# A two-layer decoder trunk: a second buffer for gathered token rows, the returned rows joined earlier, a fixed GpSimd order, and no filler matmuls

## The chip, the cores and the metric

The kernel runs on one core of a Trainium2 chip. Its time is the device time of one execution in microseconds (us). The engines of the core are named as the profile names them: PE is TensorE (matmuls; PEld its weight loads), DVE is VectorE, ACT is ScalarE, POOL is GpSimd, SP is SyncE. Each engine works through its own list of instructions in order, and an instruction waits on semaphores that other engines or DMA transfers raise.

## What is computed

Two layers over 256 tokens of width 1024, all in float32. Each layer mixes tokens (layer 0: a gated linear recurrence and attention to a fixed memory; layer 1: stick-breaking attention and the same kind of memory attention), then applies a mixture of experts; after each half comes a residual and a LayerNorm:

```python
for layer in range(2):
    mixed = concatenate([seq_out, mem_out])                 # token mixing
    x = layer_norm(ALPHA * x + mixed @ w_o[layer])
    # experts: a group of 4 is chosen, then 2 experts of its 4
    h = silu(x @ w_gate) * (x @ w_up)                       # 16 experts, 1024 -> 256
    y = einsum('tef,efd->td', h * gates[:, :, None], w_down)
    x = layer_norm(ALPHA * x + y)
```

## The kernel before

All weights lie in one table of 1 MB chunks. SP issues one DMA per chunk in a fixed order into a ring of buffers; further buffers join the ring where other tiles die (`stream.open(names, end)`; "o1" is one of them). PE has nearly always something to multiply, so the other engines' work is placed beside it.

**Experts.** `Moe.run` goes through 16 experts in eight pairs, p = 0 to 7, with 64 slots for tokens per expert, so a pair fills 128 rows. For each pair: the rows of its tokens are there (pair 0: made by matmuls; pairs 1 to 7: fetched from a copy `zd` of the normalised tokens in DRAM by an indirect DMA on POOL, L633, into the single tile `zg`); PE turns them (L743, tile `xgp`); `gu` multiplies them by the gate and up weights (L762); ACT and DVE form `h` (L809, L811); PE turns `h` (L832, tile `ht`); `po` multiplies by the down weights (L846). The results of pairs 0 to 4 (p < AWAY) go to a DRAM table `hd` by an indirect DMA on POOL (L716, "send"), those of pairs 5 to 7 are kept in `hl` and put to their tokens by matmuls (L771, tile `y`). When pair 6 is at work, each token's rows are read back from `hd` (L711, "bring"): its first into `r`, its second into `second`, 128 tokens at a time; both tiles are set to zero before, and POOL adds them (L803). After pair 7 DVE joins `r` to the residual (L868), and the last norm begins with `y` added to it (L366).

**A branch.** Between `h` and `ht` of pair 7 stands a test whether an expert has more than 64 tokens (`beyond`, L456). The engines all pass through it; the code in it is not run with these inputs. After the test PE waits for DVE's count that stands behind DVE's last instruction ahead of the test, as the trace names it `DVEq L456`.

**Order.** Inside the stages DVE, PE and ACT follow the program's order. On POOL a scheduler places the instructions that are not pinned. Before the first partition broadcast (L353, of a norm's gain and bias to all partitions) and before the first arithmetic instruction after one, POOL's list holds an instruction "ISA" which the trace calls MODIFY_POOL_CONFIG.

**The ends of the token mixing.** `mixer_end` normalises the tokens, stores them to `zd` from ACT's DMA queue (both halves), and computes who goes where; then `idx`, and the first `fetch`. `keep_busy` puts matmuls of no use on PE: 18 at the start of the program, 2, 4 and 4 at the end of layer 1's mixing, 11 between the layers (`into_next`). In layer 0's mixing, DVE doubles a decay table level by level (`double`, L1120 to L1122) and splits weights (`ag`, L220), and PE makes scores of blocks of 128 (L1165).

Of the kernel before, what the change touches and what calls it, by code (L numbers as in the profile page):

```python
# [7 lines left out]
F32 = mybir.dt.float32  # L8
# [34 lines left out]
def trunk(ctx: ExitStack, tc: tile.TileContext, w_all, x_tok_d, cst_d, msk_d, rw_d, rb_d,  # L43
# [87 lines left out]
    def keep_busy(ps, n):  # L131

        for _ in range(n):
            tc.keep_in_program_order(nc.tensor.matmul(ps, onesb, onesb[:, None, :].to_broadcast([P, 4, P]), start=True,
                                                      stop=True, skip_group_check=True))

# [50 lines left out]
    class Parts:  # L187


        def __init__(self):  # L190
            self.use("wa", "wb", "wd")

# [24 lines left out]
        def lo(self, p, src, j, scale=None):  # L217
            s = slice(j * 512, (j + 1) * 512)
            if scale is None:
# [128 lines left out]
    def rows(which, name):  # L348
# [3 lines left out]
        for v in range(2):  # L352
            nc.gpsimd.partition_broadcast(gb[:, v], gb[0:1, v])  # L353
# [45 lines left out]
    def affine(dst, z, gb, norms=None):  # L399

        for t in range(NT):
# [105 lines left out]
    class Moe:  # L507
# [16 lines left out]

        def turn_in(self, s, t, hk):
# [90 lines left out]
        def indices(self):  # L616
# [10 lines left out]

            self.zg = self.work.tile([P, D], F32, tag="zg", name=f"zg{l}")
            nc.gpsimd.memset(self.zg, 0.0)
            self.fetch(1)  # L630

        def fetch(self, p):
            nc.gpsimd.indirect_dma_start(out=self.zg, out_offset=None, in_=self.zd,  # L633
# [76 lines left out]
        def bring(self, dst, i, t):  # L710
            nc.gpsimd.indirect_dma_start(out=dst, out_offset=None, in_=self.hd,  # L711
                                         in_offset=bass.IndirectOffsetOnAxis(ap=self.back[:, i, t:t + 1], axis=0),
                                         bounds_check=ROWS - 1, oob_is_err=False)

        def send(self, p, src):
            nc.gpsimd.indirect_dma_start(out=self.hd, out_offset=bass.IndirectOffsetOnAxis(ap=self.own[:, p:p + 1], axis=0),  # L716
                                         in_=src, in_offset=None, bounds_check=ROWS - 1, oob_is_err=False)
# [19 lines left out]
        def transpose_rows(self, p):  # L737
            l = self.l
            xg = self.work.tile([P, NK, P], F32, tag="xg", name=f"xg{l}", bufs=2)
            for hk in range(2):  # L740
                ps = bank(f"xgp{l}", tag="m", shape=(P, 4, P))
                for k in range(4):
                    pin(nc.tensor.transpose(ps[:, k], self.zg[:, (4 * hk + k) * P:(4 * hk + k + 1) * P], ident))  # L743
# [4 lines left out]
        def run(self, x1, xg):  # L748
# [25 lines left out]
            def rows_of_next(p):  # L774
                xgs[p] = self.transpose_rows(p)
                if p < 7:
                    self.fetch(p + 1)

            for p in range(8):
# [33 lines left out]
                if p == 0:  # L813
                    self.turn(1)
                    hr = keep.tile([P, 2, D], F32, tag="u", name=f"hr{l}")
# [9 lines left out]
                if p == 7:  # L825
                    beyond(pool, self.pool, l, base, x1, self.most, self.late, y)
# [40 lines left out]
            for t in range(NT):  # L867
                nc.vector.scalar_tensor_tensor(x1[:, t], x1[:, t], ALPHA, r[:, t], op0=ALU.mult, op1=ALU.add)  # L868
# [756 lines left out]
```

## Time and profile before

| | |
|---|---|
| median of 3 runs | 535.89 us (532.68 to 543.47) |
| the profiled execution | 537.7 us, its span 535.9 us |
| mean granted TensorE clock | 0.983 |
| PE busy | 500.2 us (93% of the span) |
| DVE, ACT, POOL busy | 288.5, 228.5, 82.5 us |
| DMA | 158.88 MB, 296 GB/s mean |

Since PE is busy for 93% of the span, the profile is read from PE's timeline: each row there begins with a start time, and a bracket at its end gives PE's idle time just before it and who ended that. From there one goes to the timeline of the engine that ended it.

### The profile page before, as it was taken

Reading aid. Unit: us, or ns where it says so; the run is one execution under the profiler, and the core shown is the slowest. Engines: PE = TensorE matmul, PEld = TensorE weight load, DVE = VectorE, ACT = ScalarE, POOL = GpSimd, SP = SyncE. Lnnn points to the kernel's source line nnn. Section 1 sums busy time; section 2 is a strip of 40 time slices with the busy share of each in tenths; the row PEclk is TensorE's granted clock in tenths of the full one; section 3 lists DMA queues with packets and bytes.
Section 4 is the critical chain, followed back from the end, with each engine's and each line's share of the span. In section 5 each row is a group of like instructions: output and inputs, shape, how many; then the busy total and the mean of one; then the engine's idle time right before and its main releaser. Section 6 shows DMA issues by size and latency. Waiting matters only on the chain. (4 is left out here: it accounts for less than half of the span.)

```text
span 535.9 us, 9133 instructions
## 1 busy us (share of the span) xinstructions
PE 500.2 (93%) x3549; PEld 325.8 (61%) x3549; DVE 288.5 (54%) x667; ACT 228.5 (43%) x469; POOL 82.5 (15%) x90
## 2 busy tenths in 40 slices
PE   8999998999999889998998999999999779999992
PEld 4998898787995323333435889877787223333431
DVE  3668886657668322222138698676438522222236
ACT  4855436665453222222217565667424222222312
POOL 1100000002211101115331400000021111213431
PEclk9999999999999799999899999999999999999997
DMA  7999733354789999999985854334789999999602
GB/s 274 402 420 423 292 128 126 144 215 179 294 330 396 422 406 419 419 390 404 402 335 206 285 226 158 111 125 161 309 322 368 406 391 398 419 412 420 243 3 78
DMA packets 28009, 158.88 MB, mean 296 GB/s; under 512 B 5347, under 2 KB 5731, under 8 KB 11060
## 3 DMA queue, kind: packets, MB, share of 16 engines
q1 hardware_dynamic: 20736, 140.76, 66.3%
q10 hardware_dynamic: 2616, 8.74, 4.4%
q0 software_dynamic: 4608, 8.73, 4.3%
q8 instruction: 30, 0.49, 0.4%
q14 instruction: 19, 0.16, 0.1%
HBM read 157.88 MB, written 13.63 MB: 320 GB/s over the span
## 5 line engine op out<-in xcount | busy, mean ns | idle before, releaser
L762 PE MATMUL gu<-w,xg 128*64 128x512 f32 x512 | 119.9, 604 | 0.1
L762 PEld LDWEIGHTS gu<-w,xg 128*64 128x64 f32 x512 | 33.4, 137 | 56.3 <-issue 51.0
L846 PE MATMUL po<-w,hT 128*64 128x512 f32 x256 | 60.2, 610 | 0.1
L591 DVE TENSOR_SCALAR xg<-xgp,lnT 128x128 f32<-128x128 f32 x64 | 25.3, 409 | 51.6 <-ACT xg L593 50.2
L593 ACT ACTIVATE xg<-xgp,lnT 128x128 f32<-128x128 f32 x64 | 27.4, 457 | 55.8 <-PE xgp L743 52.0
L846 PEld LDWEIGHTS po<-w,hT 128*64 128x64 f32 x256 | 17.9, 139 | 35.2 <-issue 28.7
L853 DVE COPY hr<-po 128x512 f32<-128x512 f32 x10 | 6.9, 690 | 43.1 <-PE po L846 43.0
L743 PEld LDWEIGHTS xgp<-cst,zg 128*128 128x128 f32 x112 | 13.3, 152 | 20.0 <-issue 13.3
L633 POOL DMA_INDIRECT zg<-zd,idx x14 | 14.9, 1061 | 60.0 <-PE xgp L743 23.9
L743 PE MATMUL xgp<-cst,zg 128*128 128x128 f32 x112 | 16.7, 297 | 6.9 <-DMA zg<-zd,idx 6.7
L1215 POOL TENSOR_TENSOR rms<-rms,neghalf 128x2 f32<-128x2 f32 x6 | 4.1, 697 | 113.0 <-DVE rms L1214 113.0
L809 ACT ACTIVATE h<-gu 128x256 f32<-128x256 f32 (+1 forms) x18 | 6.3, 359 | 34.5 <-PE gu L762 34.5
L811 DVE SCALAR_TENSOR_TENSOR h<-gu,gsl,h 128x256 f32<-128x256 f32 (+1 forms) x18 | 8.0, 453 | 22.6 <-ACT h L809 22.6
L833 ACT ACTIVATE hT<-ht 128x256 f32<-128x256 f32 (+1 forms) x18 | 6.5, 360 | 31.4 <-PE ht L832 31.3
L220 DVE TENSOR_TENSOR wo<-w,wo 128x512 fp32r<-128x512 f32 x20 | 13.6, 717 | 11.0 <-ACT wo L215 11.0
L353 POOL PARTITION_BROADCAST gbm<-gbm x4 | 5.0, 1307 | 93.9 <-DMA gbm<-in_ln_dram 86.4
L851 DVE TENSOR_TENSOR hl<-po,hl 128x512 fp32r<-128x512 f32 x12 | 8.2, 689 | 20.9 <-ACT hl L850 20.9
L716 POOL DMA_INDIRECT hd<-hr,own x10 | 10.5, 1052 | 52.8 <-DVE gsl L735 47.4
L855 ACT ACTIVATE hr<-po 128x512 f32<-128x512 f32 x10 | 6.0, 597 | 23.5 <-PE po L846 23.5
L850 ACT ACTIVATE hl<-po 128x512 fp32r<-128x512 f32 x12 | 7.1, 597 | 20.7 <-PE po L846 12.9
L215 ACT ACTIVATE wo<-w 128x512 fp32r<-128x512 f32 x20 | 11.6, 629 | 9.7 <-PE wo L439 8.8
L771 PE MATMUL y<-hl,PT 128*128 128x512 f32 x48 | 14.3, 419 | 1.4 <-DVE hl L851 1.4
(458 smaller groups left out, 1329.4 us busy)
## 6 DMA issues: line engine op xcount, KB each, us to landing
w<-in_w_all_dram SPq DMA_DIRECT2D x131, 1024.0 KB, 8.1
hd<-in_w_all_dram ACTq DMA_DIRECT2D x2, 2560.0 KB, 21.6
zd<-s ACTq DMA_DIRECT2D x4, 512.0 KB, 9.1
w<-in_w_all_dram SPq DMA_DIRECT2D x6, 256.0 KB, 5.8
x_tok<-in_x_tok_dram ACTq DMA_DIRECT2D x1, 1024.0 KB, 4.8
out_dram<-z SPq DMA_DIRECT2D x4, 256.0 KB, 2.0
w<-in_w_all_dram SPq DMA_DIRECT2D x1, 512.0 KB
cst<-in_cst_dram SPq DMA_DIRECT2D x1, 233.0 KB, 10.7
```

The costliest lines, as they stand in the source:

```text
L215: self.last_hi = nc.scalar.activation(p[:, 0, s], src[:, s], AF.Copy, scale=1.0 if scale is None else scale).ins
L220: nc.vector.tensor_sub(p[:, 1, s], src[:, s], p[:, 0, s])
L591: nc.vector.tensor_scalar(xg[:, kk], ps, g, b, op0=ALU.mult, op1=ALU.add)
L593: nc.scalar.activation(xg[:, kk], ps, AF.Identity, scale=g, bias=b)
L633: nc.gpsimd.indirect_dma_start(out=self.zg, out_offset=None, in_=self.zd, in_offset=bass.IndirectOffsetOnAxis(ap=self.idx[:, p:p + 1], axi ...
L716: nc.gpsimd.indirect_dma_start(out=self.hd, out_offset=bass.IndirectOffsetOnAxis(ap=self.own[:, p:p + 1], axis=0), in_=src, in_offset=None ...
L743: pin(nc.tensor.transpose(ps[:, k], self.zg[:, (4 * hk + k) * P:(4 * hk + k + 1) * P], ident))
L762: pin(nc.tensor.matmul(gus[p][c * 64:(c + 1) * 64], xgs[p][:, kk, c * CAP:(c + 1) * CAP], ws[p][2 * kh + c][0][:, k * 512:(k + 1) * 512], ...
L771: pin(nc.tensor.matmul(y[t][h], self.PT[p][:, t], hl[:, i, s], start=(p == AWAY and i == 0), stop=(p == 7 and i == 1)))
L811: nc.vector.scalar_tensor_tensor(h[:, c], gus[p][:, 256 + c.start:256 + c.stop], self.gsl[:, p:p + 1], h[:, c], op0=ALU.mult, op1=ALU.mult)
L846: pin(nc.tensor.matmul(po[c * 64:(c + 1) * 64], hT[:, f, c * 64:(c + 1) * 64], ws[p][4 + c][0][:, f * D + hf * 512:f * D + hf * 512 + 512] ...
L851: nc.vector.tensor_sub(hl[:, 1, s], po, hl[:, 0, s])
```

## The change

- `zg` becomes two tiles of rows, made as soon as the tokens are stored. `fetch(1)` and `fetch(2)` are issued together, and `fetch(p + 2)` after the rows of p + 1 are turned.
- The second half of the tokens is stored from POOL's DMA queue and no longer from ACT's.
- POOL's instructions of the expert stage are pinned to the program's order. The broadcast for the last norm is called at p = 6, behind all four brings, and no longer at p = 5.
- The tile `r` is gone. A token's first row comes back into `zg`, whose halves are set to zero at p = 5 and p = 6; `second` has two tiles. POOL adds at p = 7, and DVE joins `zg` to the residual ahead of the branch, no longer behind pair 7.
- At p = 0, DVE does the second half of `affine` after `h`.
- In layer 0's mixing, `double`'s last level leaves out its unused product and goes ahead of the splits of `ag`; the scores of blocks of 128 come one step of the weave later.
- `keep_busy` and its calls are gone, and so is `stream.open(("o1",), ...)`; "gb" is opened to the ring up to end - 12 and not end - 18.

```diff
@@ rows
-            nc.gpsimd.partition_broadcast(gb[:, v], gb[0:1, v])
+            ins = nc.gpsimd.partition_broadcast(gb[:, v], gb[0:1, v])
+            if which % 2:
+                tc.keep_in_program_order(ins)
@@ class Moe
+        def rows_buffers(self):
+
+            self.zg = slots.tile([P, 2, D], F32, tag="o1", name=f"zg{self.l}")
+            pin(nc.gpsimd.memset(self.zg, 0.0))
@@ indices, fetch
-            self.zg = self.work.tile([P, D], F32, tag="zg", name=f"zg{l}")
-            nc.gpsimd.memset(self.zg, 0.0)
-            self.fetch(1)
+            for p in (1, 2):
+                self.fetch(p)
@@ rows_of_next
-                if p < 7:
-                    self.fetch(p + 1)
+                if p < 6:
+                    self.fetch(p + 2)
@@ run
+                    if p == 6:
+
+                        second.append(self.pool.tile([P, D], F32, tag="P1", name=f"second{l}"))
+                        self.clear(second[1])
+                        self.bring(self.zg[:, 0], 0, 0)
+                        for t in range(NT):
+                            self.bring(second[t], 1, t)
...
+                if p == 4:
+                    second = [pool.tile([P, D], F32, tag="zg", name=f"second{l}")]
+                    self.clear(second[0])
+                if p == 5:
+                    self.clear(self.zg[:, 0])
                 if p == 6:
-
+                    self.clear(self.zg[:, 1])
+                    self.bring(self.zg[:, 1], 0, 1)
+                if p == 7:
                     for t in range(NT):
-                        self.bring(r[:, t], 0, t)
-                    second = [self.zg, self.pool.tile([P, D], F32, tag="P1", name=f"second{l}")]
-                    for t in reversed(range(NT)):
-                        nc.gpsimd.memset(second[t], 0.0)
-                        self.bring(second[t], 1, t)
-                    for t in reversed(range(NT)):
-                        nc.gpsimd.tensor_add(r[:, t], r[:, t], second[t])
+                        pin(nc.gpsimd.tensor_add(self.zg[:, t], self.zg[:, t], second[t]))
...
                 if p == 7:
+                    for t in range(NT):
+                        pin(nc.vector.scalar_tensor_tensor(self.zg[:, t], x1[:, t], ALPHA, self.zg[:, t], op0=ALU.mult,
+                                                           op1=ALU.add))
                     beyond(pool, self.pool, l, base, x1, self.most, self.late, y)
...
-                if p == 5:
-                    r = slots.tile([P, NT, D], F32, tag="o1", name=f"r{l}")
-                    nc.gpsimd.memset(r, 0.0)
-            for t in range(NT):
-                nc.vector.scalar_tensor_tensor(x1[:, t], x1[:, t], ALPHA, r[:, t], op0=ALU.mult, op1=ALU.add)
@@ mixer_end
-            nc.scalar.dma_start(moe.zd[t * P:(t + 1) * P], s[:, t])
+            (nc.scalar, nc.gpsimd)[t].dma_start(moe.zd[t * P:(t + 1) * P], s[:, t])
...
-                stream.open(("o1",), end - 12)
...
+                moe.rows_buffers()
...
-                keep_busy(bank("idle", tag="m", shape=(P, 4, P)), 2)
                 moe.turn_in(s, 1, 1)
-                keep_busy(bank("idle", tag="m", shape=(P, 4, P)), 4)
...
@@ the caller of run
             if p == 0:
-                affine(x1, s, gb)
-                stream.open(("gb",), end - 18, keep)
-            if p == 5:
+                affine(x1, s, gb, ts=(0,))
+            if p is None:
+                affine(x1, s, gb, ts=(1,))
+                stream.open(("gb",), end - 12, keep)
+            if p == 6:
                 gb = rows(2 * l + 1, f"o{l}")
@@ start of the program
-        keep_busy(bank("busy", tag="y", shape=(P, 4, P)), 18)
@@ double, levels
-            nc.vector.tensor_mul((Fa, Fb)[lvl % 2][:, 0:n], F[:, :, 0], F[:, :, 1])
+            if 2 * c < P:
+                nc.vector.tensor_mul((Fa, Fb)[lvl % 2][:, 0:n], F[:, :, 0], F[:, :, 1])
+            return last
...
+        wparts.after = doubled[0]
+        def attn():
+            main = mem_attn(pool, qm, 0, [pr[:, h] for h in range(4)], mixed)
+            for n, _ in enumerate(main):
+                yield
+                if n == 1:
+                    last_level()
@@ into_next
-            keep_busy(idle, 11)
```

How POOL's list moves at the end of layer 1's expert stage. L633/L636 is a fetch, L716/L722 a send, L711/L714 a bring, "ISA" alone the MODIFY_POOL_CONFIG. Before:

```order
L353 ISA
L353 ISA gbo_4870<-gbo_4870 128x1024 x2
L716 DMA hd_118<-hr_4452,own_4494 640x1024
L633 DMA zg_4369<-zd_4125,idx_4350 128x1024
L711 DMA r_4904<-hd_118,back_4560 128x1024 x2
L800 MEMSET second_4959 128x1024
L711 DMA second_4959<-hd_118,back_4560 128x1024
L800 MEMSET zg_4369 128x1024
L711 DMA zg_4369<-hd_118,back_4560 128x1024
L803 ISA
L803 TENSOR_TENSOR r_4904<-r_4904,second_4959 128x1024
L803 TENSOR_TENSOR r_4904<-r_4904,zg_4369 128x1024
```

Now, from the last send (L722) on:

```order
L722 DMA hd_118<-hr_4409,own_4451 640x1024
L719 MEMSET zg_4238 128x1024
L714 DMA zg_4238<-hd_118,back_4517 128x1024
L714 DMA second_4754<-hd_118,back_4517 128x1024
L719 MEMSET second_4877 128x1024
L714 DMA second_4877<-hd_118,back_4517 128x1024
L719 MEMSET zg_4238 128x1024
L714 DMA zg_4238<-hd_118,back_4517 128x1024
L351 ISA
L351 ISA gbo_4921<-gbo_4921 128x1024 x2
L819 ISA
L819 TENSOR_TENSOR zg_4238<-zg_4238,second_4754 128x1024
```

The broadcast of `gbo` with its ISA has moved from ahead of the last send to between the last bring and the first addition. (The second addition follows as the next row.)

How DVE's list moves at the branch of pair 7, layer 1. Before, with the rows of the untaken code left out:

```order
L851 TENSOR_TENSOR hl_4889<-po_5004,hl_4889 128x512
L811 SCALAR_TENSOR_TENSOR h_5021<-gu_4973,gsl_4418,h_5021 128x256
L455 TENSOR_LOAD most_4416
L456 COMPARE_AND_BRANCH
...
L456 UNCONDITIONAL_BRANCH
L868 SCALAR_TENSOR_TENSOR x_4378<-x_4378,r_4904 128x1024 x2
L851 TENSOR_TENSOR hl_4889<-po_5196,hl_4889 128x512
```

Now:

```order
L871 TENSOR_TENSOR hl_4844<-po_4959,hl_4844 128x512
L827 SCALAR_TENSOR_TENSOR h_4978<-gu_4928,gsl_4375,h_4978 128x256
L844 SCALAR_TENSOR_TENSOR zg_4238<-x_4335,zg_4238 128x1024 x2
L455 TENSOR_LOAD most_4373
L456 COMPARE_AND_BRANCH
```

The two joins, which read what POOL adds, stand ahead of the branch now.

## Rows read from the trace of the kernel before

**Rows 1.** page, busy by engine; costliest group (us, mean ns | idle).

```profile
PE 500.2 (93%) x3549; PEld 325.8 (61%) x3549; DVE 288.5 (54%) x667; ACT 228.5 (43%) x469; POOL 82.5 (15%) x90
...
L762 PE MATMUL gu<-w,xg 128*64 128x512 f32 x512 | 119.9, 604 | 0.1
```

**Rows 2.** timeline of PE, program's start: start, us, work [idle <-releaser].

```profile
1.15 6.25 PE L134 MATMUL busy<-onesb 128*128 128x512 bf16 x18 [1.15 <-POOL onesb L156]
...
10.82 0.39 PE L237 MATMUL aq0p<-x,aq 128*128 128x256 f32 x1 [0.34 <-DVE x L1041]
```

**Rows 3.** timeline of PE, layer 0's mixing.

```profile
91.47 1.57 PE L1165 MATMUL h<-q,kk 128*128 128x128 f32 x12 [2.01 <-DVE kk L1121]
```

**Rows 4.** timeline of PE, then of POOL, pairs 0 and 1 of layer 0.

```profile
176.67 0.80 PE L832 MATMUL ht<-cst,h 128*128 128x128 f32 x2 [2.33 <-DVE h L811]
...
191.60 1.06 PE L743 MATMUL xgp<-cst,zg 128*128 128x128 f32 x8 [2.32 <-DMA zg<-zd,idx]
...
183.38 0.99 POOL L633 DMA_INDIRECT zg<-zd,idx  x1 [13.13 <-DVE xg L591]
```

**Rows 5.** windows of PE: stretch, us, busy (count), granted clock, DMA share, GB/s.

```profile
176.00:184.00 8.00, 7.28 (x24) 0.57 1.01 423
254.00:260.00 6.00, 6.00 (x27) 0.72 0.99 403
```

**Rows 6.** timeline of PE, then of DVE, pairs 0 and 1 of layer 1.

```profile
423.14 0.65 PE L832 MATMUL ht<-cst,h 128*128 128x128 f32 x2 [2.33 <-DVE h L811]
...
426.90 1.06 PE L743 MATMUL xgp<-cst,zg 128*128 128x128 f32 x8 [1.13 <-DMA zg<-zd,idx]
...
437.41 1.06 PE L743 MATMUL xgp<-cst,zg 128*128 128x128 f32 x8 [3.29 <-DMA zg<-zd,idx]
...
421.48 1.22 DVE L407 TENSOR_TENSOR x<-x,gbm 128x1024 f32<-128x1024 f32 x1
```

**Rows 7.** timelines of PE, ACT, POOL around the last send, layer 0.

```profile
253.75 0.27 PE L726 MATMUL ptp<-identb,P 128*128 128x128 bf16 x2 [2.08 <-DVE hl L851]
...
252.38 1.09 ACT L850 ACTIVATE hl<-po 128x512 fp32r<-128x512 f32 x2 [4.94 <-DMA hd<-hr,own]
...
241.15 2.48 POOL L353 PARTITION_BROADCAST gbo<-gbo  x2 [10.12 <-issue]
243.82 1.20 POOL L716 DMA_INDIRECT hd<-hr,own  x1 [0.20 <-ACT xg L593]
```

**Rows 8.** timeline of PE, fillers between the layers and before pair 0.

```profile
284.04 2.55 PE L134 MATMUL idle<-onesb 128*128 128x512 bf16 x11
...
409.20 1.02 PE L134 MATMUL idle<-onesb 128*128 128x512 bf16 x4
```

**Rows 9.** timeline of POOL, a broadcast and the arithmetic after it.

```profile
144.96 2.51 POOL L353 PARTITION_BROADCAST gbm<-gbm  x2 [7.42 <-DVE mv L220]
155.17 0.59 POOL L377 TENSOR_TENSOR normx<-normx,neghalf 128x1 f32<-128x1 f32 x1 [7.70 <-DVE normx L376]
```

**Rows 10.** timeline of POOL, end of layer 1's expert stage.

```profile
484.52 2.48 POOL L353 PARTITION_BROADCAST gbo<-gbo  x2 [7.86 <-issue]
...
502.35 0.99 POOL L711 DMA_INDIRECT zg<-hd,back  x1 [0.27 <-POOL zg L800]
511.05 2.36 POOL L803 TENSOR_TENSOR r<-r,second 128x1024 f32<-128x1024 f32 x1 [7.70 <-issue]
513.37 2.36 POOL L803 TENSOR_TENSOR r<-r,zg 128x1024 f32<-128x1024 f32 x1
```

**Rows 11.** timelines of PE, then DVE, pair 7 of layer 1.

```profile
518.00 0.41 PE L832 MATMUL ht<-cst,h 128*128 128x128 f32 x2 [0.47 <-DVEq L456]
...
519.27 3.65 PE L846 MATMUL po<-w,hT 128*64 128x512 f32 x16
...
516.87 0.48 DVE L811 SCALAR_TENSOR_TENSOR h<-gu,gsl,h 128x256 f32<-128x256 f32 x1 [3.33 <-ACT h L809]
518.02 2.36 DVE L868 SCALAR_TENSOR_TENSOR x<-x,r 128x1024 f32<-128x1024 f32 x2 [0.67 <-DVEq L456]
```

More of the change, by code (lines that the diff above doesn't have):

```diff
@@ L129, in bank @@
         return psum.tile(list(shape), dt, tag=tag, name=name)
[L131 to L135, printed above, removed]
     low = const.tile([P, 5, NH], F32, name="low")
@@ L191, in __init__ @@
             self.use("wa", "wb", "wd")
+            self.after = None
         def use(self, *names):
@@ L218, in lo @@
             s = slice(j * 512, (j + 1) * 512)
-            if scale is None:
+            if self.after:
+                with tc.issue_after(self.after):
+                    nc.vector.tensor_sub(p[:, 1, s], src[:, s], p[:, 0, s])
+            elif scale is None:
                 nc.vector.tensor_sub(p[:, 1, s], src[:, s], p[:, 0, s])
@@ L397, in apply, with affine @@
             nc.scalar.activation(dst, src, AF.Identity, scale=self.r, bias=self.nmr)
-    def affine(dst, z, gb, norms=None):
-        for t in range(NT):
+    def affine(dst, z, gb, norms=None, ts=range(NT)):
+        for t in ts:
             if norms:
@@ L626, in indices @@
             nc.vector.tensor_scalar(self.idx, ps, float(T), None, op0=ALU.add)
-            self.zg = self.work.tile([P, D], F32, tag="zg", name=f"zg{l}")
-            nc.gpsimd.memset(self.zg, 0.0)
-            self.fetch(1)
+            for p in (1, 2):
+                self.fetch(p)
         def fetch(self, p):
-            nc.gpsimd.indirect_dma_start(out=self.zg, out_offset=None, in_=self.zd,
+            nc.gpsimd.indirect_dma_start(out=self.zg[:, p % 2], out_offset=None, in_=self.zd,
                                          in_offset=bass.IndirectOffsetOnAxis(ap=self.idx[:, p:p + 1], axis=0),
@@ L710, in bring, with clear @@
         def bring(self, dst, i, t):
-            nc.gpsimd.indirect_dma_start(out=dst, out_offset=None, in_=self.hd,
-                                         in_offset=bass.IndirectOffsetOnAxis(ap=self.back[:, i, t:t + 1], axis=0),
-                                         bounds_check=ROWS - 1, oob_is_err=False)
+            pin(nc.gpsimd.indirect_dma_start(out=dst, out_offset=None, in_=self.hd,
+                                             in_offset=bass.IndirectOffsetOnAxis(ap=self.back[:, i, t:t + 1], axis=0),
+                                             bounds_check=ROWS - 1, oob_is_err=False))
+        def clear(self, dst):
+            pin(nc.gpsimd.memset(dst, 0.0))
         def send(self, p, src):
-            nc.gpsimd.indirect_dma_start(out=self.hd, out_offset=bass.IndirectOffsetOnAxis(ap=self.own[:, p:p + 1], axis=0),
-                                         in_=src, in_offset=None, bounds_check=ROWS - 1, oob_is_err=False)
+            pin(nc.gpsimd.indirect_dma_start(out=self.hd, out_offset=bass.IndirectOffsetOnAxis(ap=self.own[:, p:p + 1],
+                                                                                               axis=0),
+                                             in_=src, in_offset=None, bounds_check=ROWS - 1, oob_is_err=False))
         def turn(self, p):
@@ L814, in run @@
                     self.turn(1)
+                    yield None
                     hr = keep.tile([P, 2, D], F32, tag="u", name=f"hr{l}")
@@ L976, in mixer_end @@
                 stream.open(("o0",), end)
-                stream.open(("o1",), end - 12)
                 stream.open(parts[1:4:2], last_in_parts)
@@ L990, in mixer_end @@
                 z(1)
+                moe.rows_buffers()
                 moe.rank(1, norms[1])
@@ L994, in mixer_end @@
                 moe.count(1)
-                keep_busy(bank("idle", tag="m", shape=(P, 4, P)), 4)
                 moe.chosen()
@@ L1024, in add @@
             c = slice(j * 512, (j + 1) * 512)
-            norms[t].add(x1[:, t, c], x1[:, t, c], moe.y[t][j], j, 1.0)
+            norms[t].add(x1[:, t, c], moe.zg[:, t, c], moe.y[t][j], j, 1.0)
         finish(moe, work, add, norms, x1, z2, gb)
@@ L1120, in double @@
             nc.vector.tensor_mul(qv[:, :, 1], qv[:, :, 1], F[:, :, 0:1].to_broadcast([P, n, c]))
-            nc.vector.tensor_mul(kv[:, :, 0], kv[:, :, 0], F[:, :, 1:2].to_broadcast([P, n, c]))
-            nc.vector.tensor_mul((Fa, Fb)[lvl % 2][:, 0:n], F[:, :, 0], F[:, :, 1])
+            last = nc.vector.tensor_mul(kv[:, :, 0], kv[:, :, 0], F[:, :, 1:2].to_broadcast([P, n, c])).ins
+            if 2 * c < P:
+                nc.vector.tensor_mul((Fa, Fb)[lvl % 2][:, 0:n], F[:, :, 0], F[:, :, 1])
+            return last
+        doubled = []
         def levels():
@@ L1158, in levels, with last_level @@
             yield
-            double(64)
+            doubled.append(double(64))
             yield
+        def last_level():
             for hg in range(2):
@@ L1168, in levels @@
                 nc.scalar.activation(ATx[hg], ps, AF.Copy)
-            yield
         def ev_g(t, c0, n, ps):
@@ L1191, in trunk @@
         fl = proj_tok(xs, 768, ev_g, "ag")
-        weave(mem_attn(pool, qm, 0, [pr[:, h] for h in range(4)], mixed), fl, 3 / 4)
+        wparts.after = doubled[0]
[5 more added lines that the diff above has]
+                    last_level()
+        weave(attn(), fl, 3 / 4)
+        wparts.after = None
         run(fl)
@@ L1296, in into_next @@
         gT, bT = lnT[:, 2], lnT[:, 3]
-        idle = bank("idle", tag="m", shape=(P, 4, P))
         ps = [bank("z2t", shape=(P, 2, NT, P)) for _ in range(4)]
```

4 lines of the change are left out of this document (2 added, 2 removed).

## The prediction, made before the change ran

> **What bounds the kernel.** I read the page first: PE is busy for 93% of the span, and its costliest group, the gate and up matmuls, stood idle for 0.1 us in 512 instructions [rows 1]. So PE's list sets the time, and weights never kept it waiting in the experts. Then I read PE's timeline for the brackets at the ends of its rows, since only those 36 us of idle time, and matmuls that run at the lower clock, can be won. The gaps that the change touches are one in layer 0's mixing [rows 3], one at each pair 0 and before some turned rows [rows 4, 6], and one behind the last send of layer 0 [rows 7]. [...] Last come the places where the change puts something new ahead of PE: POOL's list and the branch at pair 7 [rows 9 to 11].
>
> **What it should win.**
> Layer 0's mixing. PE waited 2.01 us for `kk` at its last level [rows 3]. DVE now makes it ahead of the splits of `ag`, and the scores that read it come a step later. I follow the lists and leave 0.4 us of the gap: -1.6 (bounds 0 and -2.0). What is late next are the splits; other matmuls of the weave cover them.
>
> Pair 0. `ht` waited 2.33 us for `h` in both layers [rows 4, 6], and DVE's last instruction before `h` was an addition of the residual of 1.22 us [rows 6], which now comes behind. Nothing on PE reads that residual before the branch of pair 7. -1.2 in each layer, -2.4 (bounds 0, if ACT's silu is late next, and -4.7).
>
> The clock behind pair 0 of layer 0: 8 us at 0.57 lose 0.43 * 8 = 3.4 us [rows 5]. What PE did before it fell was to wait 2.33 us. The same wait in layer 1 [rows 6] lowered nothing, so a gap of this size need not do so; with half the gap I take the whole -3.4 (bounds 0 and -3.4).
>
> Fetched rows. With one buffer, the fetch for pair 2 goes out at 183.38, when the rows of pair 1 are turned, and PE waits for it at 191.60 [rows 4]. Now it goes out together with the one before, from then on a whole pair ahead. All three waits go: 2.32 in layer 0 [rows 4], 1.13 and 3.29 in layer 1 [rows 6], -6.7. The middle one is the first fetch, which waits for the token stores; the second store is on another queue now and is not behind the first. Its bounds are -1.1 and, if POOL's queue lands later than ACT's, about +2, a wait as long as the one in layer 0.
>
> The last send of layer 0. It was issued at 243.82, right behind a broadcast of 2.48 us that had begun after 10.12 us without work [rows 7]. ACT's `hl` writes the tile that this send reads, and waited 4.94 us for it; PE then waited 2.08 and ran at 0.72 for 6 us [rows 5, 7], 0.28 * 6 = 1.7. The broadcast has left its place ahead of the send. The send goes out 2.5 to 3.3 us earlier: -3.8 (bounds -2.1 and -3.8).
>
> Fillers of layer 1's mixing: ten at 1.02 / 4 [rows 8], 2.6 us, but the tables of who goes where come from a chain on DVE, and PE then stands idle in their place: -0.3 (bounds 0 and -2.6).
>
> These give -18.2.
>
> **What it should cost.**
> Pair 7. This is the term that decides. `ht` stands behind the branch, and it ran when DVE's sequencer had passed the branch, 0.65 us after the end of `h` at 517.35 [rows 11]. The two joins (2.36 us together) ran after that, under `po`, and nobody waited. Now they stand between `h` and the branch, and read POOL's additions. In POOL's list the broadcast lies between the last bring and the additions, with a MODIFY_POOL_CONFIG before each. What such a switch takes is read where one follows the other: POOL starts the broadcast after 7.42 us and the arithmetic behind it after 7.70 us [rows 9]; at the end of the stage it is 7.86 and 7.70, both with "issue" as the releaser, that is, nothing that the trace shows ended them [rows 10]. Before, the first of the two fell in a pair when POOL had nothing urgent, and the second ended in additions that were done at 515.73, before `h`. In before's own time, the new order gives: last bring ends 503.34; + 7.7 switch = 511.0; + 2.5 broadcasts = 513.5; + 7.7 switch = 521.2; + 2.32 + 2.36 additions = 525.9; + 1.2 second join = 527.1; + 0.65 through the branch = 527.75. `ht` was at 518.00. So + 9.75 in each layer, + 19.5 (bounds: + 2.4 a layer, if the additions are in time and only the joins count, and + 9.75). The brings' data is no part of it: in the row before, POOL's own queue needed no wait beyond the switch.
>
> [...]
>
> The clock behind it. PE then stands for about 10 us, three times its longest wait in these rows, 3.29 [rows 6]. The two falls priced above cost 3.4 and 1.7; I take 2.5 a layer, + 5 (bounds 0, and 7.2 a layer, the length of the matmuls that are left, `po`'s 3.65 [rows 11] and as much again for `y`, if they all run at half speed). [...]
>
> The start. The 18 fillers took 6.25 us, 0.347 each, where the 11 between the layers took 0.232 each [rows 2, 8]: the first ran at the lower level, and the first useful matmuls found the clock raised. Now these come first. They wait for their operands until 10.82 anyway [rows 2]; behind that PE is never idle, and what runs at half speed is lost: + 2 (bounds 0 and the 3.4 of [rows 5]).
>
> Between the layers, 11 fillers less: PE waits there for the norm, so their 2.55 us win nothing, and the clock may fall: + 1 (bounds 0 and 3.4).
>
> One chunk buffer fewer ("o1"): nothing, because the weights are ahead (idle 0.1, [rows 1]); if that cover were gone, PE would wait for a chunk of 1 MB, which at 423 GB/s [rows 5] takes 2.5 us. The added memsets and the earlier zeroing on POOL: nothing, they lie in its idle time.
>
> These give + 27.5. **Sum:** + 9.3 on the profiled execution's 537.7, its span being 535.9, that is 547.0. The median of the runs, 535.89, lies 1.8 below that execution, and so I put the time at 545.
>
> **Rivals.**
> A, the switches are off the path: POOL's code for the broadcast or the arithmetic stays loaded, or loads while POOL does the brings, and the additions are done before `h` as they were. For it: in layer 1 POOL was done at 515.73, ahead of `h`, although it switched twice in the stage. Against: the switch came with the same length at all four places, wherever it stood in the list. Then only the joins cost, 2.4 a layer; PE waits 3 us there, and a fall of the clock in one layer is priced at 2.5: -18.2 + 2 + 4.8 + 2.5 + 1 = -7.9, 528. If the clock holds too, 525. 13%.
>
> B, `ht` does not wait for the joins: it needs only `h`. For it: its operands. Against: its row names DVE's sequencer at the branch [rows 11], and DVE gets there in list order. Then pair 7 costs nothing on PE and the additions run beside `po`; the last join at 527.1 is then about 1 us behind the last `y`. -18.2 + 2 + 1 + 1 to 2 = -14, 522, faster by over 2%. 8%.
>
> C, slower by over 2%: the low clock behind the new 10 us wait lasts to the end of `po` and `y` in both layers. It decides where the fall costs more than 3.3 us a layer, 0.8 over the forecast's, since 546.6 is 1.6 above 545: 7.2 in place of 2.5 gives + 9.4, 554, and with the start's 3.4 instead of 2 it is 556. For it: the first stretch of [rows 5] holds 3.4 us lost, that is 6.9 us at the lower level, nearly as long as these matmuls. Against: the second holds 3.4 us at it. 14%.
>
> D, the second buffer wins little, because the token stores or POOL's own list hold the first fetches back, now that the send of pair 0 and two fetches share it: 4 of the 6.7 remain, 549. Against: pairs 0 to 2 leave POOL idle for 13.13 us before a fetch [rows 4]. 5%.
>
> **The numbers.** The forecast itself, 60%: 540 to 550 around 545, by the bounds of the start, the clock and the fillers. About 2% is what a measurement of this kernel tells from no change; that puts the borders at 525.2 and 546.6. The forecast's upper third is above, 20% of the whole; C and D add 19; that is 0.39 slower. B and a small part of A are below, 0.10 faster; the rest, 0.51, lies within. The range 528 to 554 takes in the forecast, D, the nearer half of A and half of C, and leaves out B, the rest of A and the top of C.
>
> **What would show it.** In the trace of the changed kernel: `ht` of pair 7 with about 10 us of idle time before it in each layer, released by DVE's sequencer; on POOL an idle time of 7 to 8 us before the `gbo` broadcast and again before the first addition, one behind the other; the joins on DVE ending just before the branch. A granted clock under 1 right behind, and at 10 to 14 us. No wait for `zg` before the turned rows of pairs 1 and 2, a wait near 1.1 before pair 0's `ht`, none behind the last send. I am wrong if POOL's additions end before `h`, if `ht` starts while a join is still to come, or if the three waits for `zg` only move.

## The result, and the profile after

Four runs of the changed kernel gave a median of 558.09 us (555.49 to 560.5), four of the kernel before 535.46. The ratio is 1.044, with a 95% interval of 1.036 to 1.052: slower by 22.6 us between the medians, where 545 had been forecast. The ratio leaves out before's run of 543.47, which counts as a slow run. The profiled execution took 559.52, its span 557.6 at a mean granted clock of 0.953, where before had 0.983.

The page of the changed kernel, with the busy time by engine, the clock in 40 slices and the costliest group, beside [rows 1]:

```profile
PE 502.1 (90%) x3510; PEld 329.3 (59%) x3510; DVE 296.3 (53%) x666; ACT 228.7 (41%) x469; POOL 85.4 (15%) x94
...
PEclk9999999999998999999977999999997899999957
...
L770 PE MATMUL gu<-w,xg 128*64 128x512 f32 x512 | 121.0, 604 | 2.4 <-DMA w<-in_w_all_dram 2.2
```

PE has 39 matmuls less (the fillers) and yet 1.9 us more of busy time: some of the work ran at a lower clock (0.50 in 283 to 286 and in 537 to 542 us). The clock is lowest in three places: in the middle and at the end, where the two expert stages end, and in slices 31 and 32 (418 to 446 us), where layer 1's mixing ends and its pair 0 begins. The gate and up matmuls now waited 2.2 us for weights.

PE's timeline of the changed kernel (start, us, work, idle time before it and who ended that):

```profile
91.26 0.91 PE L1184 MATMUL h<-q,kk 128*128 128x128 f32 x6 [0.28 <-DVE kk L1134]
92.09 1.13 PE L297 MATMUL sc<-memk,gate 64*128 64x256 f32 x4
...
176.93 0.65 PE L852 MATMUL ht<-cst,h 128*128 128x128 f32 x2 [2.04 <-DVE h L827]
...
188.36 1.09 PE L750 MATMUL xgp<-cst,zg 128*128 128x128 f32 x8
...
257.18 1.08 PE L770 MATMUL gu<-w,xg 128*64 128x512 f32 x4 [2.17 <-DMA w<-in_w_all_dram]
...
282.62 0.66 PE L852 MATMUL ht<-cst,h 128*128 128x128 f32 x2 [11.02 <-DVEq L456]
...
419.78 0.17 PE L574 MATMUL slot<-Ab,trib 128*128 128x16 bf16 x1 [2.08 <-DVE Ab L566]
420.62 0.77 PE L612 MATMUL xgp<-P,s 128*128 128x128 f32 x2 [0.68 <-DVE dl L653]
...
536.66 0.66 PE L852 MATMUL ht<-cst,h 128*128 128x128 f32 x2 [9.93 <-DVEq L456]
```

The gap of [rows 3] has shrunk to 0.28, and the wait for `zg` of [rows 4] is gone at 188.36. But `ht` of pair 0 still waits 2.04, there is a new pair of waits in layer 1's mixing (419.78, 420.62), and `ht` of pair 7 waits 11.02 and 9.93 for DVE to pass the branch, where [rows 11] had 0.47.

To see where the time went, the same instruction is looked up in both traces; the difference of its start, taken from one milestone to the next, is what a stretch lost or won. The forecast for each stretch is the sum of the prediction's terms that lie in it.

| stretch | forecast | measured |
|---|---|---|
| start to `ht` of pair 0, layer 0 (176.67, now 176.93) | -0.8 | +0.3 |
| to the turned rows of pair 7 (256.87, now 250.23) | -9.5 | -6.9 |
| to `ht` of pair 7 (276.26, now 282.62) | +9.75 | +13.0 |
| to the last `y` (283.23, now 291.56) | +2.5 | +2.0 |
| to the first `gu` of layer 1 (413.26, now 424.99) | +0.7 | +3.4 |
| to `ht` of pair 0 (423.14, now 435.46) | -1.2 | +0.6 |
| to the turned rows of pair 2 (437.41, now 446.84) | -4.4 | -2.9 |
| to `ht` of pair 7 (518.00, now 536.66) | +9.75 | +9.2 |
| to the end of the span (535.9, now 557.6) | +2.5 | +3.0 |
| sum | +9.3 | +21.7 |

The forecast of pair 7 holds in layer 1 and is 3.3 us short in layer 0; the rest of the missing 12.4 us lies in many places: gains that did not come, and a loss in layer 1's mixing that was put down as nothing.

POOL's timeline shows pair 7's chain in both layers:

```profile
253.15 1.00 POOL L714 DMA_INDIRECT zg<-hd,back  x1 [0.27 <-POOL zg L719]
262.74 2.48 POOL L351 PARTITION_BROADCAST gbo<-gbo  x2 [8.60 <-DMA w<-in_w_all_dram]
275.56 4.63 POOL L819 TENSOR_TENSOR zg<-zg,second 128x1024 f32<-128x1024 f32 x2 [10.34 <-issue]
...
416.92 0.74 POOL L913 DMA_DIRECT2D zd<-s  x1 [1.77 <-ACT s L397]
417.67 1.82 POOL L528 MEMSET zg<- 128x2048 f32 x1
...
511.09 1.00 POOL L714 DMA_INDIRECT zg<-hd,back  x1 [0.27 <-DMA w<-in_w_all_dram]
520.28 2.48 POOL L351 PARTITION_BROADCAST gbo<-gbo  x2 [8.19 <-DMA zg<-hd,back]
529.61 4.63 POOL L819 TENSOR_TENSOR zg<-zg,second 128x1024 f32<-128x1024 f32 x2 [6.85 <-issue]
```

Bring, switch, broadcast, switch, additions, one behind the other, as the forecast had it [rows 10]. The first switch took 8.60 and 8.19, the second 10.34 in layer 0 and only 6.85 in layer 1. A gap of that length stood in layer 0 of the kernel before too, ahead of its additions:

```profile
272.12 2.35 POOL L803 TENSOR_TENSOR r<-r,second 128x1024 f32<-128x1024 f32 x1 [11.25 <-DMA zg<-hd,back]
```

DVE's timeline, at three places:

```profile
277.92 4.49 DVE L844 SCALAR_TENSOR_TENSOR zg<-x,zg 128x1024 f32<-128x1024 f32 x2 [6.48 <-POOL zg L819]
...
417.11 2.40 DVE L565 TENSOR_SCALAR og<-rk 128x4 f32<-128x4 f32 x1
...
433.45 0.33 DVE L742 TENSOR_REDUCE gsl<-ptp 64x1 f32<-64x3 f32 x2 [0.89 <-PE ptp L735]
433.80 1.23 DVE L405 TENSOR_TENSOR x<-s,gbm 128x1024 f32<-128x1024 f32 x1
435.06 0.61 DVE L827 SCALAR_TENSOR_TENSOR h<-gu,gsl,h 128x128 f32<-128x128 f32 x2
```

The two joins take 4.49 and not the 2.36 of [rows 11]: the second takes 1.2 us, but the first takes 3.35. It begins as POOL's first addition ends, runs beside the whole of POOL's second, which is done at 280.19, and ends 1.1 us after that. An operation on 128x4 elements takes 2.40 us; it ends at 419.51, POOL's memset (the row at 417.67 above) at 419.49. It began 0.56 us before the memset's row, while POOL issued the store of tokens (416.92), so either could have held it; kernel 5 tells them apart. And between the gates `gsl` and `h` there is now a multiplication of 1.23 us, the first operation of `affine`'s second half.

### The profile page after: what moved, and what is told of

Same layout as the page of the kernel before. It is cut to its first block, busy times and chain, and to the rows that moved or that the text cites. A ratio compares the mean times of both kernels' runs of the same rounds, so it can differ in the third digit from the quotient of the medians.

```text
span 557.6 us, 9048 instructions
## 1 busy us (share of the span) xinstructions
PE 502.1 (90%) x3510; PEld 329.3 (59%) x3510; DVE 296.3 (53%) x666; ACT 228.7 (41%) x469; POOL 85.4 (15%) x94
## 5 line engine op out<-in xcount | busy, mean ns | idle before, releaser
L866 PE MATMUL po<-w,hT 128*64 128x512 f32 x256 | 63.8, 642 | 0.1
L852 PE MATMUL ht<-cst,h 128*128 128x128 f32 x32 | 7.7, 315 | 25.1 <-DVEq L456 20.9
L852 PEld LDWEIGHTS ht<-cst,h 128*128 128x128 f32 x32 | 3.7, 148 | 34.8 <-issue 22.1
L722 POOL DMA_INDIRECT hd<-hr,own x10 | 10.1, 1013 | 79.2 <-DVE gsl L742 74.4
L636 POOL DMA_INDIRECT zg<-zd,idx x14 | 14.4, 1028 | 48.1 <-PE xgp L750 20.6
L779 PE MATMUL y<-hl,PT 128*128 128x512 f32 x48 | 16.1, 461 | 1.4 <-DVE hl L871 1.4
```

The lines of the kernel that those rows point to most:

```text
L636: nc.gpsimd.indirect_dma_start(out=self.zg[:, p % 2], out_offset=None, in_=self.zd, in_offset=bass.IndirectOffsetOnAxis(ap=self.idx[:, p:p ...
L722: pin(nc.gpsimd.indirect_dma_start(out=self.hd, out_offset=bass.IndirectOffsetOnAxis(ap=self.own[:, p:p + 1], axis=0), in_=src, in_offset= ...
L779: pin(nc.tensor.matmul(y[t][h], self.PT[p][:, t], hl[:, i, s], start=(p == AWAY and i == 0), stop=(p == 7 and i == 1)))
L852: pin(nc.tensor.transpose(ht[:, f], h[:, f * P:(f + 1) * P], ident))
L866: pin(nc.tensor.matmul(po[c * 64:(c + 1) * 64], hT[:, f, c * 64:(c + 1) * 64], ws[p][4 + c][0][:, f * D + hf * 512:f * D + hf * 512 + 512] ...
```

## The experiments

**1. The joins behind the branch.** Everything else of the change stays.

```diff
                 if p == 7:
-                    for t in range(NT):
-                        pin(nc.vector.scalar_tensor_tensor(self.zg[:, t], x1[:, t], ALPHA, self.zg[:, t], ...))
                     beyond(pool, self.pool, l, base, x1, self.most, self.late, y)
...
                 stream.done(ws[p][4][1], ws[p][5][1])
+            for t in range(NT):
+                pin(nc.vector.scalar_tensor_tensor(self.zg[:, t], x1[:, t], ALPHA, self.zg[:, t], ...))
```

> The changed kernel with the two joins of zg to the residual behind the branch and behind the last hl of pair 7 on DVE; POOL's list is unchanged, so its additions are as late as before. Theory (the wait of 11.0 and 9.9 us before ht of pair 7 is the joins' place ahead of the branch): that wait falls to under 1 us in both layers although the additions still end 8 to 10 us after h; the norm then waits for the joins instead, some 1 to 3 us. Clock behind ht back at full in layer 1. Time 558 - 18 = about 540. Rival (the late additions themselves bound the end, wherever the joins stand): under 5 us come back, about 554.

Measured: 539.67, ratio to before 1.0056 (1.0012 to 1.0100). PE's timeline of this kernel:

```profile
272.32 0.41 PE L849 MATMUL ht<-cst,h 128*128 128x128 f32 x2 [0.73 <-DVEq L456]
...
285.78 1.97 PE L1336 MATMUL z2t<-cst,z 128*128 128x128 f32 x8 [6.11 <-DVE z L1332]
...
515.21 0.41 PE L849 MATMUL ht<-cst,h 128*128 128x128 f32 x2 [0.46 <-DVEq L456]
```

and POOL's:

```profile
275.41 4.72 POOL L819 TENSOR_TENSOR zg<-zg,second 128x1024 f32<-128x1024 f32 x2 [9.28 <-issue]
```

The additions are as late as in the change, but `ht` no longer waits for them, and 3.8% of the time is back. So the place of the joins ahead of the branch turned the late additions into a wait. What is late now shows between the layers, as 6.11 us before `z2t`, where the change had 2.48: the joins come behind pair 7, and the late additions stretch them to 3.79 us. With the largest cost gone the kernel is still not faster than before.

**2. The broadcast one pair earlier,** the joins where the change has them.

```diff
-                stream.open(("gb",), end - 12, keep)
-            if p == 6:
+                stream.open(("gb",), end - 18, keep)
+            if p == 5:
                 gb = rows(2 * l + 1, f"o{l}")
```

> The changed kernel with the call for the last norm's gain and bias at p = 5 and not at p = 6, so that the broadcast and its MODIFY_POOL_CONFIG lie between the last send and the first bring (and "gb" open to the ring up to end - 18). The joins stay ahead of the branch. Theory (two switches and a broadcast of 18 us stand in a row behind the last bring): one switch and the broadcast now run while POOL waits for the sends; the brings come about 3 us later; additions end near h + 1; ht of pair 7 waits about 3 us in place of 11.0 and 9.9. Time about 540. Rival (one switch alone is long enough, or POOL's bring is the bound): the wait stays over 7 us, time over 550.

Measured: 543.9, ratio 1.0130 (1.0063 to 1.0198). `ht` of pair 7 waits 6.44 and 5.62, more than the 3 us of the theory; PE's and POOL's rows of this kernel:

```profile
276.10 0.66 PE L852 MATMUL ht<-cst,h 128*128 128x128 f32 x2 [6.44 <-DVEq L456]
...
522.32 0.66 PE L852 MATMUL ht<-cst,h 128*128 128x128 f32 x2 [5.62 <-DVEq L456]
```

```profile
269.03 2.34 POOL L819 TENSOR_TENSOR zg<-zg,second 128x1024 f32<-128x1024 f32 x1 [10.26 <-issue]
...
515.24 2.35 POOL L819 TENSOR_TENSOR zg<-zg,second 128x1024 f32<-128x1024 f32 x1 [8.48 <-issue]
```

One switch and the broadcast out of the chain win 3.1% of before's time, the difference of the two ratios. The rest of the wait is the second switch, which is still behind the last bring, and the two joins at 4.49 us, as in the change.

**3. The memset of `zg` later,** called ahead of the fetches.

```diff
 rows_buffers:
-            pin(nc.gpsimd.memset(self.zg, 0.0))
 indices, ahead of the fetches:
+            pin(nc.gpsimd.memset(self.zg, 0.0))
```

> The changed kernel with the zeroing of the 128x2048 tile of rows put behind idx, just ahead of the first two fetches, and no longer behind the token store. Theory (POOL's memset holds DVE's TENSOR_SCALAR at L565: 2.40 and 1.39 us in place of 0.17): L565 is 0.17 us again in both layers, the waits of PE before slot (2.08 and 0.57) go, and the clock in layer 1's pair 0 is full. Fetches 1 us later at most. Time 558 - 6 = about 552. Rival (the token store from POOL's queue, which ran at the same time, holds DVE): L565 still over 0.6 us in layer 1. Rival 2 (the fillers taken out at this place are what is missing): L565 is short but the clock still falls here; under 3 us come back.

Measured: 559.55, ratio 1.0396 (1.0322 to 1.0470). It tests nothing: in POOL's list the memset stands where it stood, right behind the store of the tokens, the short operation at L564 takes 2.40 us still, and PE still waits 2.08 for `slot`. Kernel 5 tries the other direction.

**4. `h` ahead of the rest at pair 0.**

```diff
+                    ins = nc.vector.scalar_tensor_tensor(h[:, c], ...)
                 if p == 0:
-                    self.turn(1)
+                    with tc.issue_after(ins.ins):
+                        self.turn(1)
```

> The changed kernel with pair 0's h ahead of the gates of pair 1 and of the whole second half of affine on DVE. Theory (the predicted gain at pair 0 failed because the first multiplication of that half, 1.23 us, stands between the gates and h): ht of pair 0 waits under 1 us in place of 2.04 in both layers, and the clock does not fall behind it in layer 0. Time 558 - 3 to 4 = about 554 to 555. Rival (ACT's silu sets the time of h): the wait stays at 2 us, no change.

Measured: 552.51, ratio 1.0267 (1.0204 to 1.0330). `ht` of pair 0 waits 0.78 and 0.80. PE's timeline and a window (stretch, us, busy and count, granted clock, DMA share, GB/s) of this kernel, and the same window of the change:

```profile
176.86 0.65 PE L853 MATMUL ht<-cst,h 128*128 128x128 f32 x2 [0.78 <-DVE h L827]
...
434.00 0.65 PE L853 MATMUL ht<-cst,h 128*128 128x128 f32 x2 [0.80 <-DVE h L827]
```

```profile
178.00:186.00 8.00, 8.00 (x42) 1.00 1.01 411
...
178.00:186.00 8.00, 8.00 (x34) 0.81 1.01 413
```

The clock behind pair 0 of layer 0 is full, where the change has 0.81 in the same stretch and before 0.68 (0.57 from 176 to 184 us, [rows 5]). So the multiplication was what kept the gain at pair 0 away. The shorter wait and the full clock go together: over all the traces here, both layers, the clock fell behind pair 0's `ht` in 12 of 18 cases with a wait of 2.0 to 2.3 us, and in none of 6 with one of 0.8 (kernels 4, 8 and 10). Not all of the 1.7% between the two ratios can come from here: in this kernel's profiled execution, the slowest of its five, `ht` of pair 7 in layer 0 starts at 282.63, as in the change, because POOL's chain sets it.

**5. The memset earlier,** on top of kernel 1: `rows_buffers` is called ahead of `z(1)` in both mixings.

```diff
-                z(1)
                 moe.rows_buffers()
+                z(1)
```

> The kernel with the joins behind the branch (e1_joins_behind), and the zeroing of the tile of rows called ahead of the second token store, so that POOL does it while it waits for that store's data. (e3_memset_late had left POOL's list as it was.) Theory (the memset holds DVE's TENSOR_SCALAR L565): L565 takes 0.17 us in both layers, PE's waits before slot (2.08 in layer 1, 0.58 in layer 0) go, and layer 1's pair 0 runs at the full clock; 5 us less than e1_joins_behind, about 535. Rival 1 (the store's issue on POOL holds DVE): L565 stays over 0.6 us in layer 1. Rival 2 (what lacks is the ten fillers): waits short, but the clock is still low at layer 1's pair 0, under 2.5 us less.

Measured: 537.33, ratio 1.0018 (0.9985 to 1.0051). POOL's and DVE's rows of this kernel:

```profile
406.12 1.80 POOL L528 MEMSET zg<- 128x2048 f32 x1
```

```profile
408.15 0.17 DVE L565 TENSOR_SCALAR og<-rk 128x4 f32<-128x4 f32 x1
```

With the memset done, the same operation takes 0.17 instead of 2.40, though POOL issues the store beside it (407.95 to 408.69), and PE's wait for `slot` is gone. From the last `lg` matmuls to the first `gu` of layer 1 PE now needs 6.90 us, where kernel 1 needed 10.02 and the kernel before, with its fillers, 6.88: so the memset made the loss there, and not the store or the missing fillers. The full clock at pair 0 did not come: it was 0.83 in 420 to 430 us, behind the wait of 2.04 for `h`, and instead of the 5 us of the theory some 2 came back. The trace shows the cause; that gain over kernel 1, 0.4% of before's time, is within the two intervals and so not shown by the times.

**6. The kernel before without its fillers,** all calls of `keep_busy` left out and nothing else changed.

> The kernel before, without any of its fillers (18 at the start, 11 between the layers, 10 in layer 1's mixing), nothing else changed. Theory (the fillers bring nothing measurable, and the changed kernel loses in layer 1's mixing by its memset, not by its missing fillers): same time, 0 to + 1.5 us, about 537; no wait over 1 us and no low clock ahead of pair 0 of layer 1. Rival (the fillers hold the clock): a low clock at the start, between the layers or at pair 0 of layer 1, + 3 to + 6 us, about 541.

Measured: 537.54, ratio 1.0004 (0.9968 to 1.0040). The fillers were worth nothing that can be measured, though without them the clock is 0.83 in 280 to 290 us where it was 1.00.

**7. One more chunk buffer less:** the changed kernel with `RING = 8` instead of 9.

> The changed kernel with 8 ring buffers for weights in place of 9. Theory (PE's wait of 2.17 us for weights in pair 6 of layer 0 comes from the one buffer that the change took from the weights): one chunk less ahead, of about 3 us in this stretch, so the wait grows to about 5 us there or one more like it comes earlier; the wait of ht of pair 7 shrinks by what the brings gain. Rival (DMA alone sets the pace of the weights, however many buffers wait for them): the wait stays at 2 us +- 0.5.

One run: 557.67, the time of the change. PE's timeline:

```profile
257.61 1.04 PE L770 MATMUL gu<-w,xg 128*64 128x512 f32 x2 [2.88 <-DMA w<-in_w_all_dram]
260.83 1.97 PE L770 MATMUL gu<-w,xg 128*64 128x512 f32 x4 [2.17 <-DMA w<-in_w_all_dram]
...
282.69 0.66 PE L852 MATMUL ht<-cst,h 128*128 128x128 f32 x2 [4.75 <-DVEq L456]
```

The waits for weights grow from 2.17 to 5.05, so the number of buffers makes them. `ht` of pair 7 starts at the same time, 282.69 and 282.62, with a shorter wait: what PE loses ahead of it costs nothing there, since POOL's chain ends last.

**8. Together:** kernels 1, 4 and 5, the additions on DVE, and the two halves of each score matmul kept side by side.

```diff
+                        ins = nc.tensor.matmul(scs[c][:, t], ...)
+                        if c:
+                            tc.keep_in_program_order(ins)
...
-                        pin(nc.gpsimd.tensor_add(self.zg[:, t], self.zg[:, t], second[t]))
+                        pin(nc.vector.tensor_add(self.zg[:, t], self.zg[:, t], second[t]))
```

> The changed kernel with what the runs so far point to: joins behind the branch, memset ahead of the second store, pair 0's h ahead of the gates of pair 1, the additions of the returned rows by DVE ahead of pair 7's h (so POOL needs no second switch before the branch), and the score matmuls of the memory attention kept in pairs. Theory: from e1_joins_behind's 540, - 5 (memset), - 3 (h), - 1.5 to 2 a layer (additions no longer late), - 1 (pairs), + 2.5 (PE is earlier, so it waits longer for weights in layer 0): about 529, faster than the kernel before by 1 to 1.5%. Rival (weights bound layer 0 and eat what is won there): 533 to 536, the same as before.

Measured: 534.78, ratio 0.9953 (0.9921 to 0.9985): below before by half a per cent, and the lowest ratio of the kernels here. It is not the 529 of the theory, but in the rival's range; PE waits 1.14 and 2.01 us for weights in layer 0. PE's timeline of this kernel, in the mixing and at the end of layer 0:

```profile
95.74 1.13 PE L297 MATMUL sc<-memk,gate 64*128 64x256 f32 x8
...
268.78 0.41 PE L852 MATMUL ht<-cst,h 128*128 128x128 f32 x2 [0.74 <-DVEq L458]
...
280.80 1.54 PE L1339 MATMUL z2t<-cst,z 128*128 128x128 f32 x6 [4.68 <-DVE z L1335]
```

Eight score matmuls take 1.13 us in the place where the change took 1.13 for four. A wait of 4.68 is left between the layers, for the joins and the statistics of the norm, which follow each other on DVE.

**9. Traffic under the second switch:** the changed kernel, with eight more chunk loads at pair 7 of layer 1 that nobody reads.

```diff
+                if p == 7 and l == 1:
+                    for i in range(8):
+                        extra = ringp.tile([P, CH], F32, tag="w", name=f"extra{i}")
+                        nc.sync.dma_start(extra, w_all[i])
```

> The changed kernel with eight more weight chunks (8 MB, never used) loaded at pair 7 of layer 1, when otherwise the DMA engines stand idle (share 0.02 there, 1.00 at the same place of layer 0). Theory (a switch of POOL's code takes 9.4 to 11.2 us in layer 0 and 6.9 to 7.6 in layer 1 because its code comes over the same DMA engines as the weights): MODIFY_POOL_CONFIG to the first addition takes over 9 us in layer 1 too, and ht of its pair 7 waits 12 to 14 us in place of 9.9. Rival (the length comes from what POOL does before it, or from the code that is loaded): it stays at 7 to 7.6 us. The total time is of no use here, since the stores of the output queue behind these loads.

One run, of use for its trace alone. POOL's timeline and its windows:

```profile
523.12 2.48 POOL L351 PARTITION_BROADCAST gbo<-gbo  x2 [8.55 <-issue]
...
536.82 2.33 POOL L823 TENSOR_TENSOR zg<-zg,second 128x1024 f32<-128x1024 f32 x1 [11.22 <-issue]
```

```profile
526.00:536.50 10.50, 0.00 (x0) 0.75 1.02 420
```

The same in the changed kernel without the extra loads, layer 0 and layer 1:

```profile
265.50:275.50 10.00, 0.00 (x0) 1.00 1.01 388
...
523.00:529.50 6.50, 0.00 (x0) 0.98 0.01 3
```

The second switch of layer 1 takes 11.22 instead of 6.85 once the DMA engines are full, as it does in layer 0 where they are full anyway (10.34). The first switch, ahead of the broadcast, hardly changed: 8.55 at a DMA share of 1.02, 8.19 at 0.73. `ht` of pair 7 then waits 14.94.

**10. Kernel 8 with fillers put back:** 22 between the layers, 2, 4 and 4 in layer 1's mixing.

> e8_combined with fillers put back where its PE waits: 22 between the layers (its wait there is 4.68 us, and the granted clock 0.70 in the ten us behind it) and 2, 4 and 4 in layer 1's mixing (0.83). Theory: the clock stays full in both places, 3 to 4 us less than e8_combined, about 531. Rival (PE in those stages waits for the norm's chain on DVE and ACT, so a faster clock wins nothing): as e8_combined, 534 to 535.

Measured: 534.9, ratio 0.9976 (0.9948 to 1.0005), against 0.9953 without them, with overlapping intervals. The clock was full in both places (1.00 in 280 to 290 and in 400 to 410 us, where kernel 8 had 0.70 and 0.83), and no gain from it can be measured, here either.

## Why the prediction was wrong

The sign was the forecast's, and so was the mechanism at pair 7; the size was not: 21.7 us more in the profiled executions, where 9.3 was forecast. No single term makes up the missing 12.4. One step was wrong in kind (the memsets, put at nothing), one large cost was mis-sized (pair 7 of layer 0, 3.3 short), and most of the gain at pair 0 did not come. Step by step:

- **Pair 7, right in its mechanism, too low in layer 0.** From the last bring to `ht` the forecast had 24.4 us; the change took 28.5 in layer 0 (254.15 to 282.62) and 24.6 in layer 1 (512.09 to 536.66). Layer 0 was mis-sized by switches of 8.60 and 10.34 instead of 7.7 each, 3.5 us together, and by joins that ended 2.2 us behind the additions instead of 1.2. The forecast took 7.7 from four places, none of them in layer 0's expert stage; there the kernel before had gaps of 10.12 ahead of the broadcast, in the forecast's own [rows 7], and of 11.25 ahead of the additions. In layer 1 the sum held in part by luck: one switch was longer than 7.7 (8.19), the other shorter (6.85). Kernels 1 and 2 confirm both halves, the branch and POOL's chain. Rival A fell: the switches stayed on the path, 6.85 to 10.34 long. Rival B fell with the row at 282.62. Kernel 9 shows that the second switch's length goes with the traffic beside it, 6.85 against 11.22 us; that a switch loads code for POOL, and over the DMA engines, as A and that kernel's theory take it, is a supposition that no trace shows.
- **The clock behind it, right:** +2.0 and +3.0 for 2.5 each, so not C. Its lower level, half speed, is a granted clock of 0.50 in the traces: from 177 to 183 us in the kernel before, from 283 to 286 and from 537 to 542 in the change.
- **"The added memsets and the earlier zeroing on POOL: nothing, they lie in its idle time", the step that failed.** POOL was idle there, but DVE was not: it stood for as long as POOL's memset ran. The tables of who goes where stand behind that operation; PE waited 2.08 us for them in layer 1, and 0.57 in layer 0, where the operation took 1.39. (The 0.68 behind the wait of layer 1 is not the memset's: kernel 5 has 0.71 there, and the kernel before has a filler in its place.) In layer 1 PE then worked at a clock of 0.66 from 420 to 430 us:

```profile
420.00:430.00 10.00, 9.22 (x54) 0.66 0.54 213
```

  Forecast for that stretch up to `gu` +0.7, measured +3.4, all of it behind the last `lg` (10.24 us from there to `gu`, 6.88 before); the slow clock took the gain of pair 0 behind it as well. Kernel 5, with the memset earlier, has 6.90 there. The traces show that one engine holds the other, and price it, 2.40 for 0.17 us; by what means, they do not show.
- **Pair 0, -1.2 each, wrong:** -0.3. The addition of `affine`'s second half left its place between the gates `gsl` and `h`, but the multiplication of that half came into it (433.80, 1.23 us), and `h` still stands behind the gates of pair 1. I had seen one addition ahead of `h` in before [rows 6] and taken the instruction that left for the wait that would go. Kernel 4 shows the 1.25 that was still to be had.
- **The clock behind pair 0 of layer 0, -3.4, wrong:** a wait of 2.04 stayed, and behind it the clock fell again. 0.81 for 8 us loses 1.5; kernel 4 has no fall. In layer 1 the same wait lowered nothing in the kernel before, but here it did.
- **Fetched rows, right:** all three waits are gone, D with them. Layer 1's two waits were worth 2.9 in the table instead of 4.4, because the clock behind pair 0 lies in the same stretch (0.63 from 436 to 440 us).
- **The last send, right:** PE's wait behind it is gone.
- **Layer 0's mixing, -1.6, half wrong.** The gap closed by 1.73. But in the kernel before, the score matmuls on 64 rows ran in pairs, eight in 1.14 us; the weave now put the halves of one group apart, and they took 1.13 us for four (the row at 92.09 above). It gave back about 1.1.
- **"One chunk buffer fewer: nothing", wrong in its reason:** weights were late by 2.17 us at 257.18. The forecast's own price was 2.5 if the cover went. It cost nothing only because pair 7 waited longer (kernel 7).
- **Fillers, wrong at the start.** [rows 2] was read as if PE had nothing useful to do until 10.82. In the kernel before its first useful matmul began at 7.05, and in the change at 6.19; the first ones took longer there (0.41 us for 0.28), but by the first `h` of layer 0's mixing the two kernels were level (87.84 and 87.64). The +2 was thus nothing, and the gains missed in the table's first stretch are some 3 us and not 1.1. All fillers together, with those of layer 1's mixing, were priced at +2.7; kernel 6 has all those of the kernel before at +0.2, at most +2.1 by its interval.

What stays open: why kernel 4's time is lower by more than its gaps explain, what makes a switch to the broadcast 7.9 us in one place and 10.1 in another, and how much of kernel 8's 0.5% is due to which of its edits; they were not run one by one.

## What to carry to other kernels

An idle engine is not free room: look at what another engine does in the same microseconds, and at what its result holds up; here a memset of 1.82 us in POOL's idle time cost PE a wait of 2.08. An instruction placed ahead of a branch that all engines pass can delay work behind the branch that does not need it: `ht` of pair 7 waited 11.02 and 9.93 us with the joins ahead of it, 0.73 and 0.46 with them behind it (kernel 1). And before a wait is booked as won, list all that stands between the last input and the waiting operation; taking one of two instructions away may win little, 0.3 of 1.2 us at pair 0.

## What the runs showed of the hardware

- A POOL memset of 128x2048 held a DVE operation on 128x4 elements until it was done (0.17 became 2.40 us, in layer 1 of the change), and beside a POOL addition of 128x1024 a DVE join of that size took 3.35 us instead of 1.2. Other small DVE operations beside the memset kept their length (0.16 to 0.25 us each in kernel 5).
- POOL's switch from the broadcast to arithmetic took 6.85 us with the DMA engines idle (share 0.01, the change) and 11.22 with them full (1.02, kernel 9), at the same place in the program; in layer 0, where the share was 1.01 in the change, it took 9.28 to 10.78 in the change and in kernels 1 to 3.
- Matmuls on 64 rows took half the time where the two halves of the rows stand side by side in PE's list: eight in 1.13 us (kernel 8), against four in 1.13 where they do not (the change).
- The kernel before took the same time without its 39 filler matmuls as with them, as far as can be measured (ratio 1.0004, 0.9968 to 1.0040).
